# Hybrid decoder step: state, key, query and decay rows loaded through ScalarE's DMA queue

## The chip, the cores and the metric

The kernel runs on one core of a Trainium2 chip. The metric is the device time of one execution in microseconds (us); the median of the runs shown is compared. The engines are named as in the profile: PE (TensorE's matmuls), PEld (its weight loads), DVE (VectorE), ACT (ScalarE), POOL (GpSimd) and SP (SyncE, which here does nothing but issue DMAs). Each engine works through its own list of instructions in order; an instruction that waits for a semaphore holds everything behind it on that engine.

## What is computed

One layer of a decoder for 256 prompt positions and 8 sample sequences with one new token each (264 columns in all), followed by a final norm. Cut to what matters:

```python
h = rms_norm(x, norm_w)
z = h @ w_in                      # 4096 -> 14368 columns
# A: dilated window attention, 8 heads; B: trailing-mean pooling; C: gated delta rule, 16 heads
# C, prompt: chunked form, decay[i, j] = exp(gc[i] - gc[j]), gc = cumsum of the log decay
# C, sample: one step of the recurrence, for each of 8 samples and 16 heads
state = state * exp(g)
delta = (v - k @ state) * beta
state = state + outer(k, delta)
o     = q @ state
y = x + concat(A * silu(gA), B * silu(gB), C * silu(gC)) @ w_out
```

The caches and states are outputs too: the window cache is copied with one row replaced, and the new 128 x 128 state of each sample and head is written back.

## The kernel before

**The stream.** The 112 column tiles of `w_in`, a small one for the decays, and the 32 column tiles of `w_out` stream through PE one after the other. A chunk is 8 of a tile's 32 row blocks. Its weights arrive in one of three buffers `raw` (a load of 1 MB holds two chunks); ACT casts them to a high part `wh` (`emit_split`, L498, `s.copy`), DVE subtracts to get the low part `wl`, and PE runs three matmuls of 264 columns per row block (`emit_main`, L531, with the matmuls in L550 to L552), 24 for a chunk. There are four pairs `wh`/`wl` (`HB = 4`), so the cast for chunk n+3 stands in the program behind the matmuls of chunk n and waits until PE has left the buffer of chunk n-1. When DVE has read the last chunk of a `raw` buffer, the next load is put on SP's queue (`emit_loads`, L466), often followed by a piece of the cache copy, 512 KB from HBM to HBM (`emit_copy`, L486).

**The work beside it.** Everything else is written as Python generators that give up control at each `yield`: evacuations of finished tiles, the attention heads, the pooling, and of part C the keys' products (`kk`, L747), two `delta_worker`s that take the 16 prompt heads in turn (`delta`, L925), and two `sample_worker`s that take the 32 half heads of the samples (`sample`, L1063: four samples of one head each). Between two chunks `step` (L1417) picks the generators whose next piece fits, and the pieces' instructions are put into the engines' lists at that place. Matmuls of this side work are collected (`put`, L322) and given to PE in the middle of a chunk once they count as ready (`flush`, L330).

**The planner.** What fits is decided on a model of the engines' clocks (`Model`, L75; `Meter`, L144). It holds a time for PE, DVE, ACT, POOL and SP and one for the DMA engines, taken as one first-come queue (`Model.dma`, L132: SP gives 0.46 us to an issue, the transfer starts 0.65 us later at the earliest and behind all earlier ones, runs at 359 KB/us and counts as landed 0.9 us after its end). `ready` (L103) is the time at which an access's earlier readers and writers are done. The order of all engines' work is therefore fixed when the program is built.

**The loads of the change.** `send` (L298) yields until the model's time for the buffer and source is no later than PE's, then issues on SP:

```python
while not self.free and self.model.ready([out], [in_]) > self.model.t["pe"]:
    yield
self.sy.dma_start(out=out, in_=in_)
```

`load_decay` (L736) loads one head's row of `s_gc` to all 128 partitions (128 KB); `kk` uses it 16 times and `delta` 16 times. `sample` loads for each half head the states `sdT` (256 KB) into `Sb`, and a row of `s_k` and one of `s_q` to all partitions (256 KB each) into `kb` and `qb`. Each sample worker has one set of these buffers: a new state can only be loaded when the store `o_ds` of the previous one has landed, a new key row when DVE has read the last. After the loads, `due` (L293) yields until the model expects the last of them within 0.5 us; then come DVE's products with the keys. The stores (`o_ds`, `o_dp`, `s_q`), the weights, the copies and the attention's loads (`kg`, `vg`) also go through SP. All DMAs of SP and ACT share eight completion semaphores in turn, in the order of the program, and the framework lets an issue wait for the DMA that used its semaphore before.

Of the kernel before, what the change touches and what calls it, by code (L numbers as in the profile page):

```python
# [11 lines left out]
P = 128  # L12
NP = 256
# [177 lines left out]
class Builder:  # L191
# [106 lines left out]
    def send(self, out, in_):  # L298

        while not self.free and self.model.ready([out], [in_]) > self.model.t["pe"]:  # L300
            yield
        self.sy.dma_start(out=out, in_=in_)

    def pause(self, n):
        for _ in range(n):
            yield
# [427 lines left out]


    def load_decay(self, h, gcb):  # L736
        yield from self.send(gcb.ap, self.s_gc[h:h + 1, :].to_broadcast([P, NP]))

    def decay(self, h, gcb, D):

# [322 lines left out]
    def sample(self, h, f, Sb, kb, qb, jk, sm):  # L1063
        yield from self.wait(("q", h), ("v", h))
        n = NB // 2
        if f == 0:
            yield from self.send(self.s_q[h].rearrange("f d b -> d f b"),
                                 self.qall[:, h * NB:(h + 1) * NB].rearrange("d (f b) -> d f b", f=2))
        yield from self.send(Sb.ap, self.d["sdT"][h, :, f * 512:(f + 1) * 512])
        yield from self.send(kb.ap, self.s_k[h, f:f + 1].rearrange("f d b -> f (d b)").to_broadcast([P, 512]))  # L1070
        yield from self.send(qb.ap, self.s_q[h, f:f + 1].rearrange("f d b -> f (d b)").to_broadcast([P, 512]))
        yield from self.due(self.loaded)
        S = Sb.ap.rearrange("p (b k) -> p b k", b=n)
        k = kb.ap.rearrange("p (k b) -> p b k", b=n)
        q = qb.ap.rearrange("p (k b) -> p b k", b=n)
        junk = [jk.ap[:, i * P:(i + 1) * P] for i in range(4)]
        c0 = h * NB + f * n
        hs = slice(c0, c0 + n)
        eg, a1, a2 = (self.stab.ap[:, i * P + c0:i * P + c0 + n] for i in range(3))
        kS, dl = sm.ap[:, 0:n], sm.ap[:, n:2 * n]  # L1080
        for b in range(n):
            self.stt(junk[b], S[:, b], 1.0, k[:, b], ALU.mult, ALU.mult, accum=kS[:, b:b + 1])
            if b % 2:
                yield
                for j in (b - 1, b):
                    self.act(S[:, j], S[:, j], AF.Copy, scale=eg[:, j:j + 1])
        self.tt(dl, self.vall[:, hs], a2, ALU.mult)
        self.tt(kS, kS, a1, ALU.mult)
        self.tt(dl, dl, kS, ALU.subtract)
        yield  # L1090
        for b in range(n):
            self.stt(S[:, b], k[:, b], dl[:, b:b + 1], S[:, b], ALU.mult, ALU.add)
        yield
        for b in range(n):
            self.stt(junk[b], S[:, b], 1.0, q[:, b], ALU.mult, ALU.mult, accum=self.oall[:, c0 + b:c0 + b + 1])
        yield
        yield from self.send(self.d["o_ds"][h, :, f * 512:(f + 1) * 512], Sb.ap)
        self.ndone += 1
        if self.ndone == 2 * CH:
            self.start(self.sample_end())  # L1100
# [672 lines left out]
```

## Time and profile before

| | before |
|---|---|
| median of 3 runs | 1829.66 us (1829.58 to 1832.16) |
| the profiled execution | 1833.11 us |
| its span, first to last instruction | 1831.3 us |
| granted clock, mean share | 0.992 |
| PE busy | 1800.3 us (98%) |
| DVE / ACT / POOL busy | 1299.7 (71%) / 853.3 (47%) / 192.6 us (11%) |
| moved by the DMA engines | 519.13 MB, mean 283 GB/s |
| SP's hardware queue (q1) | 516.18 MB, 81.3% of the engines' time |
| ACT's hardware queue (q10) | 0.02 MB, 0.0% |

The page gives busy shares over the whole span. Where a stage lasted longer than its work is read from the windows, from the timeline of one engine (an idle time stands in brackets behind the instruction that ended it, with what it waited for), and from the lists of waits. SP is never counted as busy: its issues stand with the time that the issue took, and a wait of SP is one of its list.

### The profile page before, as it was taken

The page shows a single profiled execution, that of the slowest core. Times are in us where ns is not written, and L with a number is a line of the kernel's source. Part 1 is how long each engine was busy: PE and PEld are TensorE (multiplying, and loading weights), DVE is VectorE, ACT ScalarE, POOL GpSimd, SP SyncE. Part 2 cuts the span into 40 slices and gives each one's busy share as a digit, 9 for nine tenths or more (in the row PEclk, how much of TensorE's full clock was granted, in tenths as well). Part 3 has the DMA queues.
Part 4 walks back from the last instruction along what each step waited for, and adds up shares of the span by engine and source line. Part 5 has one row for each costly group of instructions (what it writes and reads, how often), then busy time and mean ns, then how long its engine had stood idle before and what let it go on. Part 6 is the DMA issues. An engine that isn't in the chain of part 4 may idle for free.

```text
span 1831.3 us, 38119 instructions
## 1 busy us (share of the span) xinstructions
PE 1800.3 (98%) x15122; PEld 1786.2 (98%) x15122; DVE 1299.7 (71%) x3157; ACT 853.3 (47%) x1439; POOL 192.6 (11%) x504
## 2 busy tenths in 40 slices
PE   9999999999999999999999999999999999999996
PEld 8999999999999999999999999999999999999995
DVE  7987889767888888888777876667655654444444
ACT  6744444445455555455544443444333444444442
POOL 1121454430111111110000000000000000000000
PEclk9999999999999999999999999999999999999998
DMA  8788778666889899889888887779888798888873
GB/s 305 267 313 281 266 247 240 232 205 226 277 269 326 287 300 306 291 293 297 313 304 319 323 293 270 287 277 344 313 296 288 264 344 306 305 296 308 298 241 118
DMA packets 109379, 519.13 MB, mean 283 GB/s; under 512 B 25408, under 2 KB 36256, under 8 KB 70272
## 3 DMA queue, kind: packets, MB, share of 16 engines
q1 hardware_dynamic: 108624, 516.18, 81.3%
q8 instruction: 118, 1.93, 0.4%
q0 software_dynamic: 432, 0.50, 0.1%
q14 instruction: 61, 0.50, 0.1%
q10 hardware_dynamic: 144, 0.02, 0.0%
HBM read 499.14 MB, written 152.50 MB: 356 GB/s over the span
## 4 chain that ended last, share of the span: by engine, by line
PE 83%; DVE 7%; DMA 7%; issue 1%; ACT 1%; SPq 1%; DVEq 0%; ACTq 0%
PE mps L550 25%; PE mps L551 25%; PE mps L552 25%; DVE arena L174 4%; PE sps L316 4%; DVE wl L174 2%; DMA o_ds<-arena 2%; DMA arena<-s_gc 1%; DMA raw<-win 1%; DMA arena<-vg 1%; PE sps L320 1%; PE sps L551 1%; PE sps L550 1%; PE sps L552 1%; SPq L158 1%
## 5 line engine op out<-in xcount | busy, mean ns | idle before, releaser
L550 PE MATMUL mps<-xh,wh 128*128 128x264 f32 x3456 | 998.6, 289 | 1.4 <-ACT wh L174 1.4
L551 PE MATMUL mps<-xl,wh 128*128 128x264 f32 x3456 | 982.3, 284 | 0.0
L552 PE MATMUL mps<-xh,wl 128*128 128x264 f32 x3456 | 981.5, 284 | 0.0
L174 DVE TENSOR_TENSOR wl<-raw,wh 128x1024 fp32r<-128x1024 f32 (+1 forms) x581 | 704.2, 1213 | 390.3 <-ACT wh L174 388.3
L174 ACT CAST wh<-raw 128x1024 fp32r<-128x1024 f32 (+1 forms) x581 | 603.6, 1040 | 601.4 <-PE mps L551 530.3
L550 PEld LDWEIGHTS mps<-xh,wh 128*128 128x128 f32 x3456 | 654.0, 189 | 4.7 <-ACT wh L174 2.7
L551 PEld LDWEIGHTS mps<-xl,wh 128*128 128x128 f32 x3456 | 653.5, 189 | 0.2
L552 PEld LDWEIGHTS mps<-xh,wl 128*128 128x128 f32 x3456 | 650.5, 188 | 0.2 <-DVE wl L174 0.2
L174 DVE SCALAR_TENSOR_TENSOR arena<-arena 128x128 f32<-128x128 f32 (+5 forms) x882 | 264.5, 354 | 22.1 <-DMA arena<-s_k 18.5
L174 ACT ACTIVATE arena<-arena 128x128 f32<-128x128 f32 (+6 forms) x319 | 118.7, 400 | 148.5 <-DVE arena L174 147.8
L550 PE MATMUL mps<-mixc,wh 128*128 128x264 f32 x512 | 145.5, 284 | 0.0
L550 PE MATMUL mps<-mix,wh 128*128 128x264 f32 x512 | 145.5, 284 | 0.0
L551 PE MATMUL mps<-mix,wh 128*128 128x264 f32 x512 | 145.1, 283 | 0.0
L551 PE MATMUL mps<-mixc,wh 128*128 128x264 f32 x512 | 145.1, 283 | 0.0
L552 PE MATMUL mps<-mixc,wl 128*128 128x264 f32 x512 | 145.0, 283 | 0.0
L552 PE MATMUL mps<-mix,wl 128*128 128x264 f32 x512 | 145.0, 283 | 0.0
L174 POOL COPY arena<-arena 128x8 f32<-128x8 f32 (+5 forms) x192 | 69.2, 380 | 462.3 <-DVE arena L174 377.1
L551 PEld LDWEIGHTS mps<-mixc,wh 128*128 128x128 f32 x512 | 96.5, 188 | 0.0
L551 PEld LDWEIGHTS mps<-mix,wh 128*128 128x128 f32 x512 | 96.5, 188 | 0.0
L550 PEld LDWEIGHTS mps<-mixc,wh 128*128 128x128 f32 x512 | 96.4, 188 | 0.0
L550 PEld LDWEIGHTS mps<-mix,wh 128*128 128x128 f32 x512 | 96.4, 188 | 0.0
L552 PEld LDWEIGHTS mps<-mix,wl 128*128 128x128 f32 x512 | 96.0, 187 | 0.0
(111 smaller groups left out, 1321.1 us busy)
## 6 DMA issues: line engine op xcount, KB each, us to landing
raw<-win SPq DMA_DIRECT2D x214, 1024.0 KB, 5.4
o_wk<-ck SPq DMA_DIRECT2D x128, 511.8 KB, 8.2
o_wv<-cv SPq DMA_DIRECT2D x128, 511.8 KB, 6.9
raw<-wout SPq DMA_DIRECT2D x58, 1024.0 KB, 5.4
arena<-kg SPq DMA_DIRECT2D x32, 320.0 KB, 7.0
arena<-vg SPq DMA_DIRECT2D x32, 320.0 KB, 8.0
arena<-sdT SPq DMA_DIRECT2D x32, 256.0 KB, 8.2
arena<-s_k SPq DMA_DIRECT2D x32, 256.0 KB, 7.8
```

What stands on the lines that cost most here:

```text
L158: return f(*a, **k)
L174: return f(*a, **k)
L316: self.put(lambda: self.t.matmul(out, lhsT=lhsT, rhs=rhs, start=start, stop=stop), out, [lhsT, rhs], 2)
L320: self.put(lambda: self.t.transpose(out, in_, self.ident[:k, :k]), out, [in_], 1)
L550: self.t.matmul(ps, lhsT=h[:, w], rhs=xh, start=(k == 0), stop=False)
L551: self.t.matmul(ps, lhsT=h[:, w], rhs=xl, start=False, stop=False)
L552: self.t.matmul(ps, lhsT=l[:, w], rhs=xh, start=False, stop=(k == NK - 1))
```

## The change

A new method `fetch` stands beside `send`. It yields under the same condition but issues on ACT's queue and keeps the model's books for that: ACT's clock goes to the time at which the buffer is ready plus 0.1 us, the transfer joins the model's one DMA queue as before, and `loaded` is the later of the queue's end plus 0.9 us and ACT's clock plus 4.0 us. `load_decay` and the three loads of `sample` call `fetch`; the store of `s_q` and all else stay on SP. The change touches 128 DMAs: 32 each of `s_gc`, `sdT`, `s_k` and `s_q`.

```diff
+    def fetch(self, out, in_):
+
+        m = self.model
+        while not self.free and m.ready([out], [in_]) > m.t["pe"]:
+            yield
+        self.s.dma_start(out=out, in_=in_)
+        m.t["s"] = max(m.t["s"], m.ready([out], [in_])) + .1
+        n = 4
+        for x in out.shape:
+            n *= x
+        m.t["dma"] = max(m.t["dma"], m.t["s"] + .65) + n / 359e3
+        self.loaded = max(m.t["dma"] + .9, m.t["s"] + 4.0)
+        m.done(self.loaded, [out], [in_])
 ...
     def load_decay(self, h, gcb):
-        yield from self.send(gcb.ap, self.s_gc[h:h + 1, :].to_broadcast([P, NP]))
+        yield from self.fetch(gcb.ap, self.s_gc[h:h + 1, :].to_broadcast([P, NP]))
 ...
-        yield from self.send(Sb.ap, self.d["sdT"][h, :, f * 512:(f + 1) * 512])
-        yield from self.send(kb.ap, self.s_k[h, f:f + 1].rearrange("f d b -> f (d b)").to_broadcast([P, 512]))
-        yield from self.send(qb.ap, self.s_q[h, f:f + 1].rearrange("f d b -> f (d b)").to_broadcast([P, 512]))
+        yield from self.fetch(Sb.ap, self.d["sdT"][h, :, f * 512:(f + 1) * 512])
+        yield from self.fetch(kb.ap, self.s_k[h, f:f + 1].rearrange("f d b -> f (d b)").to_broadcast([P, 512]))
+        yield from self.fetch(qb.ap, self.s_q[h, f:f + 1].rearrange("f d b -> f (d b)").to_broadcast([P, 512]))
```

## Rows read from the trace of the kernel before

**Rows 1.** The page, part 1: busy time, share of the span, instructions

```profile
PE 1800.3 (98%) x15122; PEld 1786.2 (98%) x15122; DVE 1299.7 (71%) x3157; ACT 853.3 (47%) x1439; POOL 192.6 (11%) x504
```

**Rows 2.** Windows: length, busy us (instructions) of five engines, PEclk, DMA share, GB/s

```profile
400.00:1000.00 600.00, 589.96 (x4871) 585.88 (x4870) 480.36 (x1429) 308.47 (x651) 54.77 (x163) 0.99 0.87 292
1400.00:1800.00 400.00, 400.00 (x3306) 399.73 (x3305) 205.04 (x241) 175.24 (x223) 0.00 (x0) 1.00 0.81 287
```

**Rows 3.** Timeline of PE: start, us, instruction [idle before, releaser], five places

```profile
436.93 0.49 PE L316 MATMUL sps<-arena 128*128 128x128 f32 x2 [0.65 <-DVE arena L174]
...
485.68 0.94 PE L316 MATMUL sps<-arena,kt 128*128 128x128 f32 x4 [3.18 <-ACT arena L174]
...
765.48 0.44 PE L320 MATMUL sps<-small,arena 128*128 128x128 f32 x2 [2.70 <-DVE arena L174]
...
875.97 0.53 PE L320 MATMUL sps<-small,arena 128*128 128x128 f32 x2 [0.62 <-DVE arena L174]
...
954.60 0.83 PE L320 MATMUL sps<-small,arena 128*128 128x128 f32 x3 [1.54 <-ACT arena L174]
```

**Rows 4.** Windows of 5 us behind the idle time at 485.68

```profile
485.00:490.00 5.00, 4.32 (x23) 4.32 (x24) 3.48 (x14) 3.30 (x10) 0.30 (x1) 0.66 0.33 92
490.00:495.00 5.00, 5.00 (x44) 5.00 (x44) 4.96 (x17) 3.41 (x7) 0.00 (x0) 1.00 0.77 295
```

**Rows 5.** Timeline of DVE: waits for loads, four places

```profile
431.18 1.14 DVE L174 SCALAR_TENSOR_TENSOR arena<-arena 128x128 f32<-128x128 f32 x4 [2.09 <-DMA arena<-s_gc]
...
483.32 0.38 DVE L174 SCALAR_TENSOR_TENSOR arena<-arena 128x128 f32<-128x128 f32 x1 [2.25 <-DMA arena<-s_k]
...
688.28 0.39 DVE L174 SCALAR_TENSOR_TENSOR arena<-arena 128x128 f32<-128x128 f32 x1 [2.14 <-DMA arena<-s_k]
...
761.34 0.39 DVE L174 SCALAR_TENSOR_TENSOR arena<-arena 128x128 f32<-128x128 f32 x1 [3.89 <-DMA arena<-s_k]
```

**Rows 6.** Waits: engine, line, releaser: us in total, times, longest

```profile
DVE arena L174 <- DMA arena<-s_k: 18.5, 13, 3.9
```

**Rows 7.** DMA issues: queue, count, KB each, median us from issue to landing

```profile
arena<-s_k SPq DMA_DIRECT2D x32, 256.0 KB, 7.8
...
arena<-cmask POOLq DMA_DIRECT2D x1, 64.0 KB, 10.4
```

**Rows 8.** SP's issues: ns min/median/max of the issue, first and last start

```profile
L158 SPq DMA_DIRECT2D arena<-s_gc x32: 319/572/1420, 115.8 to 805.2; - x32
L158 SPq DMA_DIRECT2D arena<-sdT x32: 328/388/1217, 415.9 to 978.7; - x32
L158 SPq DMA_DIRECT2D arena<-s_k x32: 320/455/1842, 416.6 to 979.7; - x32
L158 SPq DMA_DIRECT2D arena<-s_q x32: 319/430/1384, 424.2 to 980.9; - x32
```

**Rows 9.** Waits of SP for landings: us in total, times, longest

```profile
SPq L158 <- DMA raw<-win: 32.5, 27, 3.0
SPq L158 <- DMA o_ds<-arena: 25.1, 15, 6.5
...
SPq L158 <- DMA o_wk<-ck: 13.8, 14, 2.2
```

**Rows 10.** The chain that ended last: start, us, what

```profile
414.69 7.34 DMA o_wk<-ck
422.05 9.10 DMA arena<-s_gc
```

**Rows 11.** Waits of ACT: the longest in total

```profile
ACT wh L174 <- PE mps L551: 530.3, 330, 2.8
```

**Rows 12.** Timeline of SP and of ACT around one load of a state

```profile
744.09 0.58 SPq L158 DMA_DIRECT2D o_ds<-arena  x1
...
753.23 0.33 SPq L158 DMA_DIRECT2D arena<-sdT  x1
...
751.24 1.05 ACT L174 CAST wh<-raw 128x1024 fp32r<-128x1024 f32 x1 [1.85 <-PE mps L551]
```

## The prediction, made before the changed kernel ran

> **What bounds the kernel now.** I read the page first. PE is busy for 1800.3 of 1831.3 us [rows 1], so whatever the change does must show in PE's idle time or in the pace of its matmuls. Next come windows by stage, to find where PE is not busy. From 1400 to 1800 us, where only the stream is left, PE is busy for all of 400 us; from 400 to 1000 us, where the delta heads and the samples run beside the stream, it lacks 10.0 of 600 us [rows 2]. The rest of the missing time lies ahead of the first matmul and behind the last, where no load of the change runs. The third view is the timeline of PE between 400 and 1000 us. It shows that the 10 us are a few holes, and five of them make 8.7 us: 0.65 + 3.18 + 2.70 + 0.62 + 1.54 [rows 3]. Each ends at a small matmul of the side work that waits for DVE or ACT; none ends at a matmul that waits for weights. After a long hole there is a second loss: in the 5 us behind 485 us the granted clock is 0.66, that is the lower of the two levels (1.2 GHz) for about 3.4 us, after PE had stood idle for 3.18 us; PE finishes 23 matmuls there against 44 in the next 5 us [rows 4]. Of that, 0.68 us is still the hole, and 3.4 us at half speed cost 1.7 us more. The hole of 2.70 us at 765 us looks the same and is put at 1.7 us too.
>
> Then the timeline of DVE says why. DVE waited 2.25 us for a key row just ahead of the hole at 485.68, 3.89 us ahead of the one at 765.48, and 2.09 us for decays at 431.18, ahead of the one at 436.93 [rows 5]. In total DVE waited 18.5 us for key rows, in 13 waits [rows 6]. DVE is 80% busy in this stretch [rows 2], so a late load pushes everything behind it, and the planner has put a matmul in PE's list for a time that no longer holds. Not every wait costs: 2.14 us at 688.28 is followed by no hole [rows 3, 5].
>
> So what the change can win is bounded: the five holes and two slow stretches, 8.7 + 3.4 = 12.1 us, against 1833.11 us of the profiled execution (span 1831.3 and 1.8 us around it). That execution lies 3.4 us (0.19%) above the median of 1829.66 us, and I carry the difference over to the median.
>
> **The change part by part.** *The loads leave SP's queue.* A key row lands 7.8 us after its issue [rows 7], for 256 KB that at the mean 292 GB/s [rows 2] are 0.9 us of transfer; the rest is mostly time behind weights and copies that SP issued earlier. On ACT's queue they no longer stand in that line. How soon they then land no row shows. Bounds: not below about 1 us for the transfer itself; not above what the one row of a second queue shows beside a busy SP queue, 10.4 us for 64 KB [rows 7]. I take 5 to 6 us, between the ends, because the 7.8 us are the nearest row (same size, same form) and a load would pass part of that line. The waits to be removed are 2 to 4 us long, so two or three us suffice. *They can also be issued earlier.* SP reaches a place in the program after ACT does, since it first waits for DVE to release weight buffers. At 753.23 SP issued a state load; ACT had finished its work ahead of that place before the cast at 751.24, and stood idle 1.85 us [rows 12]. I count three quarters of the 12.1 us as won: **-9.0 us** (ends 0 and -12.1). What is late next is DVE itself, with 80% busy.
>
> *128 issues on ACT.* On SP an issue takes a median of 0.57, 0.39, 0.46 and 0.43 us for the four kinds [rows 8], together 32 x 1.85 = 59 us; at the maxima, 1.2 to 1.8 us, a group of three takes 4.4 us. ACT is busy for 308 of 600 us in the stretch [rows 2]. The model gives it 0.1 us for each, so some 1.0 us per group of three comes unplanned. The cover is ACT's wait for PE ahead of a cast, 530.3 us in 330 waits, 1.6 us each [rows 11]; three median issues (1.27 us) fit into it where no evacuation stands between. If they don't, a small matmul waits for the evacuation. I take **+1 us** (ends 0 and +5).
>
> *New waits on ACT.* The loads carry their waits with them. Behind a waiting issue stand the casts of the weights, so DVE's subtraction and the stream, and the evacuations that delta's next matmul waits for. Three kinds of wait come. One is the buffer: at 753.23 SP had waited for the store issued at 744.09 [rows 12]; ACT would have stood there too, and the cast of 751.24 would have come two us later or more. SP waited 25.1 us in 15 waits for such stores, the longest 6.5 us [rows 9]. The second is the completion semaphore: SP's decay load at 422.05 was released by the landing of a cache copy issued at 414.69 [rows 10], which nobody reads and which is the eighth issue before it. SP waited 32.5 us for landed weights and 13.8 us for copies, 41 waits [rows 9], mostly of this kind; the model knows nothing of them, and ACT, which comes to the place earlier than SP, meets them earlier. The third is DVE's last read of a key row; the model knows that, and `fetch` lets ACT's clock wait for it. What a held us costs has no row. Bounds: 0, as for the 2.14 us at 688.28; and 0.65, which is what DVE's 18.5 us of waits cost (12.1 / 18.5). ACT has more room than DVE, 49% idle against 20%, so I scale: 0.65 x 20 / 49 = 0.27 per us. The 25.1 us for stores would cost 6.7 us; the model foresees about half, since it too lets ACT wait for the modelled landing: **+3.4 us** (ends 0 and 0.27 x 71.4 = +19.3, all three waits of rows 9).
>
> *SP is relieved* of 59 us of issues and of the waits at them. Weights then go out a little earlier. No hole waited for weights [rows 3], so this counts 0. The s_q store stays on SP in front of a load on ACT; the order is kept by a wait, of the third kind. The bytes are the same, and the DMA engines have 13% left in the stretch [rows 2].
>
> *The order of the work changes.* The model moves every generator that comes after a changed `loaded`, so holes will not stand where they stood. I give this no sign; it adds some us to both sides of the range.
>
> **Sum:** -9.0 + 1 + 3.4 = -4.6 us: 1833.1 becomes 1828.5 for an execution like the profiled one, and the median 1829.66 becomes **1825.0 us**, 0.25% faster.
>
> **The rivals.** *The loads come no earlier* (no change). A load on ACT's queue shares the DMA engines, 87% busy [rows 2], and is held by the same buffers and semaphores. For it speaks the 64 KB on POOL's queue that took 10.4 us [rows 7]; against it that a lone row, for a software queue, decides little. Then the holes stay and the costs are small: -1 + 1 = 0, 1829.7 us. The Trainium skill, "DMA: Bandwidth & Descriptors", section "Issuing engines are not separate DMA queues", says that transfers from several engines run on the same 16 DMA engines and interleave, and that issuing from more of them saves only issue time; by that rule this rival holds, and the trace agrees as far as the POOL row goes. The same page, section "Queues, rings and completion order", lets each DMA engine take turns between the rings that have work, and by that the loads would pass part of SP's line; no row here shows ACT's ring under load.
>
> *ACT held* (slower). The waits of rows 9 now hold casts and evacuations. Place: 415 to 980 us, and at the densest where both sample workers load together. Price: 71.4 us x 0.27 = 19.3 us; less the 9.0 us won, +10 us: 1840 us. It decides as soon as a held us costs over 0.13 us (9.0 / 71.4). For it: the semaphore waits are unplanned. Against it: the casts are ready early, ACT waits for PE ahead of 330 of them [rows 11]. A milder form, half the price, is 1830 us, no change.
>
> *The change does not issue the loads earlier*, because ACT waits where SP waited: the first rival's time.
>
> **How the numbers follow.** A change under 0.2% (3.7 us) can't be told from none for this kernel. The forecast has 0.45, all of it faster by over 0.2%, 1816 to 1826 us; no change 0.28, from 1826 to 1833.3; ACT held 0.27, above. The lower end leaves out only a full win of all 12.1 us: 1817. The upper end takes in the slower case but for its upper part: 1838. Where the forecast holds, its own range is 1817 to 1826 us.
>
> **What would show it.** Right: 128 issues in ACT's queue, about 28 MB in its hardware queue; DVE's waits for key rows well below 18.5 us; landing times under 7.8 us; PE's holes between 400 and 1000 us down from 10 us to about 4, and no stretch of that part at the lower clock. Wrong: holes that end at evacuations by ACT, with ACT waiting in its queue for landings of stores, copies or weights for 40 us or more; casts that come so late that the stream's own matmuls wait; or landing times as before.

## The result and the profile after the change

| | before | after |
|---|---|---|
| median | 1830.91 us (4 runs) | **1856.14 us** (1852.61 to 1863.73, 4 runs) |
| ratio, 95% interval | | **1.0142** (1.0105 to 1.0179) |
| the profiled execution | 1833.11 us | 1863.73 us |
| PE idle in 400 to 1000 us | 10.0 us | 32.0 us |
| DVE's waits for the four kinds of load | 20.9 us in 15 | 3.5 us in 2 |
| ACT's idle time that ended at an issue or a landing | 10.9 us in 9 | 96.0 us in 30 |
| SP's waits for landings of these loads | 7.3 us in 13 | 128.1 us in 42 |

The change made the kernel 25 us slower; 4.6 us faster had been forecast. (The ratio is that of the means. The three rows of waits are sums over the lists of waits between 100 and 1040 us, each from one profiled execution; that of the changed kernel is the slowest of its four, 0.4% above their median.) The loads did move to ACT's queue, as the page's part on queues shows (packets, MB, share of the 16 engines):

```profile
q1 hardware_dynamic: 90192, 486.81, 74.7%
q10 hardware_dynamic: 18576, 29.38, 5.6%
```

The windows of after, beside [rows 2] and [rows 4], say where the time went: in the same 600 us PE gets through 4620 matmuls where it had done 4871, and behind a hole the granted clock is 0.50, the lower level.

```profile
400.00:1000.00 600.00, 568.02 (x4620) 562.02 (x4619) 456.71 (x1353) 290.99 (x625) 60.83 (x160) 0.98 0.83 274
520.00:525.00 5.00, 4.27 (x19) 3.97 (x20) 3.93 (x13) 0.87 (x3) 1.63 (x5) 0.50 0.76 247
```

PE is idle for 21.9 us more than before, and by the trace's record of the granted clock it runs at the lower level (half speed) for 23.9 us of this stretch instead of 6.8, which costs another 8.5. The sum, 30.5 us, is nearly the whole distance of 30.6 us between the two profiled executions. By the releasers, 14.7 of the 32.2 us of holes that PE has in its list of waits between 100 and 1040 us end at ACT, the others at DVE. The timeline of PE has more long holes than [rows 3]; four of them:

```profile
520.73 0.48 PE L334 MATMUL sps<-small,arena 128*128 128x128 f32 x1 [4.96 <-DVE arena L174]
...
595.33 0.58 PE L330 MATMUL sps<-arena,kt 128*128 128x128 f32 x1 [3.19 <-ACT arena L174]
...
683.61 0.55 PE L330 MATMUL sps<-arena 128*128 128x128 f32 x1 [2.45 <-ACT arena L174]
...
827.99 0.47 PE L334 MATMUL sps<-small,arena 128*128 128x128 f32 x1 [3.60 <-DVE arena L174]
```

The lists of waits of DVE, ACT and SP between 100 and 1040 us answer to [rows 6], [rows 11] and [rows 9] (us in total, times, longest):

```profile
DVE arena L174 <- DMA arena<-s_k: 3.5, 2, 3.0
...
ACT arena L174 <- issue: 30.9, 8, 8.0
ACT wh L174 <- issue: 20.2, 8, 8.2
...
ACT wh L174 <- DMA arena<-s_k: 9.1, 2, 5.5
ACT arena L174 <- DMA o_wk<-ck: 8.1, 2, 6.5
...
SPq L158 <- DMA arena<-s_gc: 60.5, 14, 9.2
SPq L158 <- DMA arena<-sdT: 38.0, 12, 17.2
...
SPq L158 <- DMA arena<-s_q: 22.4, 9, 4.3
...
SPq L158 <- DMA arena<-s_k: 7.2, 7, 3.6
```

In the same stretch of the kernel before, these were all the idle times of ACT that ended at an issue or a landing, and the largest of SP's waits for the four kinds of load:

```profile
ACT wh L174 <- issue: 7.8, 6, 1.4
...
ACT wh L174 <- DMA raw<-win: 3.1, 3, 1.5
...
SPq L158 <- DMA arena<-s_k: 2.9, 3, 1.3
```

DVE hardly waits for keys any more. In exchange ACT stands idle until issues have gone out, and, what the prediction did not have at all, SP stands waiting for loads that ACT issues. ("issue" is the page's word for idle time before which the engine waited for nothing that the profile shows; in the places below, issues of loads stand in it.) The row that names o_wk<-ck is to be read with care: its longest, 6.48 us up to 680.92, was a state load held until 678.16, and what had landed at 678.08 was the store o_ds issued at 669.89; the list names the copy that happened to land last.

Two pieces of the chain of waits show both kinds (start, us, what):

```profile
412.99 4.32 DMA arena<-s_k
...
417.38 0.34 SPq L158
...
418.34 9.75 DMA s_q<-small
...
428.17 0.33 ACTq L158
428.54 0.67 ACTq L158
...
429.25 0.38 ACT arena L174
...
429.67 0.71 PE sps L330 x4
...
805.82 9.24 DMA o_ds<-arena
...
815.08 0.34 ACTq L158
815.46 1.61 ACTq L158
...
817.16 1.43 ACTq L158
818.63 1.06 ACT wh L174
819.71 1.23 DVE wl L174
...
827.99 1.11 PE sps L334 x4
```

From 805.82 on it is ACT alone: the store of a state takes 9.24 us to land, ACT's next state load waits for it, the issues of key and query behind it take 1.61 and 1.43 us, and only then come the cast, behind the longest of ACT's idle times that ended at an issue (8.2 us), and DVE behind it. From 412.99 on it goes through both lists: ACT's key load has to land before SP may use its completion semaphore again (417.38), so SP issues the store of the queries late (418.34), ACT's query load waits for that store (428.17), and an evacuation and PE wait for ACT.

### The profile page after: what moved, and what is told of

Its sections match the earlier page's. It is cut to its first block, busy times and chain, and to the rows that moved or that the text cites. A ratio compares the mean times of both kernels' runs of the same rounds, so it can differ in the third digit from the quotient of the medians.

```text
span 1861.9 us, 38130 instructions
## 1 busy us (share of the span) xinstructions
PE 1808.6 (97%) x15122; PEld 1792.5 (96%) x15122; DVE 1299.6 (70%) x3157; ACT 849.6 (46%) x1439; POOL 201.5 (11%) x504
## 4 chain that ended last, share of the span: by engine, by line
PE 82%; DMA 8%; DVE 7%; ACT 1%; issue 1%; ACTq 1%; SPq 0%; POOL 0%; DVEq 0%; POOLq 0%
PE mps L564 25%; PE mps L565 25%; PE mps L566 24%; DVE arena L174 4%; PE sps L330 4%; DMA o_ds<-arena 4%; DVE wl L174 2%; DMA arena<-s_k 1%; PE sps L334 1%; ACTq L158 1%; PE sps L565 1%; PE sps L564 1%; PE sps L566 1%; ACT wh L174 1%; DMA s_q<-small 1%
## 5 line engine op out<-in xcount | busy, mean ns | idle before, releaser
L174 ACT CAST wh<-raw 128x1024 fp32r<-128x1024 f32 (+1 forms) x581 | 602.6, 1040 | 604.1 <-PE mps L565 484.7
L174 POOL COPY arena<-arena 128x3 f32<-128x3 f32 (+5 forms) x192 | 67.3, 370 | 466.9 <-DVE arena L174 434.9
```

The costliest lines, as they stand in the source:

```text
L174: return f(*a, **k)
```

## The experiments

| run | the 128 loads | ratio (95%) | SP's waits for ACT's DMAs | ACT idle until issue or landing | DVE's waits for loads | PE idle, 400 to 1000 |
|---|---|---|---|---|---|---|
| changed kernel | all on ACT | 1.0142 (1.0105-1.0179) | 128.1 | 96.0 | 3.5 | 32.0 |
| order_sp | SP, new order | 0.9998 (0.9983-1.0013) | 0 | 17.1 | 25.2 | 13.3 |
| queue_only | ACT, old books | 1.0159 (1.0139-1.0179) | 112.8 | 95.1 | 2.9 | 33.3 |
| kq_act | states on SP | 1.0166 (1.0147-1.0185) | 179.6 | 70.4 | 32.1 | 30.2 |
| state_act | states alone on ACT | 0.9996 (0.9984-1.0008) | 23.2 | 49.6 | 11.4 | 11.6 |
| decay_act | decays alone on ACT | 1.0122 (1.0097-1.0146) | 85.2 | 26.5 | 36.3 | 26.2 |
| samples_act | decays on SP | 1.0119 (1.0099-1.0139) | 41.2 | 73.6 | 2.4 | 24.8 |
| tiny_act | SP, 128 x 64 bytes on ACT | 1.0757 (1.0723-1.0791) | 262.2 | 57.0 | 114.2 | 86.3 |
| tiny_sp | SP, 128 x 64 bytes on SP | 1.0393 (1.0378-1.0409) | 0 | 28.1 | 62.4 | 52.2 |
| order_pool | all on POOL | 1.0070 (1.0046-1.0094) | 0 | 22.6 | 23.5 | 15.8 |
| decay_pool_same | decays alone on POOL | 1.0054 (1.0034-1.0074) | 0 | 25.2 | 24.0 | 15.4 |
| late_act | ACT, put later | 1.0089 (1.0061-1.0117) | 195.0 | 59.4 | 0.2 | 13.1 |
| kq_first | ACT, state last | 1.0128 (1.0107-1.0149) | 135.5 | 80.0 | 5.7 | 28.0 |
| soon | SP, due 2.5 us later | 0.9951 (0.9936-0.9966) | 0 | 10.4 | 2.5 | 4.2 |
| soon_state | states on ACT, due later | 0.9993 (0.9981-1.0006) | 15.7 | 50.7 | 0.3 | 12.6 |
| soon_after | ACT, due later | 1.0115 (1.0094-1.0137) | 139.5 | 82.2 | 0.0 | 25.4 |
| soon_more | SP, due 5 us later | **0.9917** (0.9900-0.9934) | 0 | 13.0 | 0.0 | 0.0 |

All ratios are to the kernel before, run beside; waits are in us, from the lists between 100 and 1040 us of one profiled execution of each run. For order_pool that was the fastest of five (1834.09 us, median 1839.81), so its row shows a milder case than its ratio. Where an expectation names 117.6 or 75 us, that was worked out otherwise, by pairing each issue with the semaphore it waits on and that semaphore's landings; the lists, which name the releaser that came last, give 128.1 for the first.

### Queue and order apart

The change does two things at once: another engine issues, and the planner books the loads otherwise, so all work gets another order. The first run keeps the new order and gives the issue back to SP; the second keeps the issue on ACT and the old books.

```diff
 # order_sp
-        self.s.dma_start(out=out, in_=in_)
+        self.nc.sync.dma_start(out=out, in_=in_)
 # queue_only
         self.s.dma_start(out=out, in_=in_)
-        m.t["s"] = max(m.t["s"], m.ready([out], [in_])) + .1
 ...
+        self.loaded = m.dma(out, in_)
```

> The changed kernel with its order of work kept for PE, DVE, POOL and ACT's own instructions, and with the 128 loads issued by SP again instead of ACT. It separates the planner's new order (and its later due time for the loads) from the queue. In the changed kernel ACT sat idle for 95.8 us between 100 and 1020 us until an issue or a landing, against 9.4 us in the kernel before; the profiled runs are 30.6 us apart. Theory A (ACT is held by the waits that the loads carry): these waits are back on SP, so ACT's idle time until an issue or a landing falls to about 10 us, PE's holes from 32.5 to about 10 us, and the time comes to 1824 to 1834 us, 0.996 to 1.002 of the kernel before. Rival C (the new order itself costs, whoever issues): it stays at 1850 to 1860 us, 1.010 to 1.016, with DVE or ACT late for the small matmuls as in the changed kernel.

> The 128 loads are issued by ACT, but the planner keeps the books as if SP issued them, so the order of all other work is that of the kernel before. Theory A (ACT is held by the waits that the loads carry): the loss is here too, and as the planner does not know of ACT's waits it is not smaller than in the changed kernel: 1.012 to 1.030 of the kernel before, ACT idle 80 us or more until an issue or a landing. Rival C (the new order costs): 0.997 to 1.003. Together with the run that has the new order on SP it makes a two by two table of queue and order.

The order alone costs nothing (0.9998), the queue alone costs the whole loss (1.0159). With the new order on SP, DVE waits 25.2 us for loads as before, so it is the queue too that makes the loads come in time. Rival C falls. Nor do the loads on ACT's queue slow the weights on SP's: worked out from the semaphores' updates, a weight load between 400 and 1000 us lands 7.0 us after its issue in the changed kernel (median), 7.4 in the kernel before.

### Which of the loads

Each run sends some of the four loads back through `send`, so the planner's order of work differs a little from run to run too:

```diff
 # kq_act: states back to SP; state_act: the three others; decay_act: the three of samples; samples_act: decays
-        yield from self.fetch(Sb.ap, self.d["sdT"][h, :, f * 512:(f + 1) * 512])
+        yield from self.send(Sb.ap, self.d["sdT"][h, :, f * 512:(f + 1) * 512])
```

> The changed kernel, but the 32 loads of states go through SP; the 96 loads of keys, queries and decays stay on ACT. Theory A1 (what holds ACT is the wait of a state load for the landing of the store that used its buffer; one such chain has a store issued at 805.82, landed after 9.24 us, the state load at 815.08 and the next cast at 818.63 after 8.19 us of idle time): without these the loss is gone for the most part, 0.997 to 1.005 of the kernel before, and ACT's idle time until an issue or a landing is 30 us or less. Rival B (each load holds ACT about alike, by its issue and by the completion semaphore that it shares with SP's DMAs): three quarters of the loss stay, 1.009 to 1.014, ACT idle about 70 us.

> The opposite part: only the 32 loads of states go through ACT, the 96 others through SP as before. Theory A1 (the wait for the store's landing): most of the loss is here, 1.008 to 1.015 of the kernel before, ACT idle 50 us or more until an issue or a landing. Rival B (each load alike): a quarter of it, 1.002 to 1.005, ACT idle some 25 us.

> Only the 32 loads of decays go through ACT; states, keys and queries go through SP as before. A decay's row waits for no store. In the changed kernel SP waited 58.2 us in 12 places for landings of decays on ACT. Theory E (coupling): SP's waits for landings on ACT are 30 us or more and the time is 1.003 to 1.008 of the kernel before. Rival S (waits for stores): 0.997 to 1.002.

> The 96 loads of the samples go through ACT, the 32 of decays through SP. Against the changed kernel this takes away the 58.2 us that SP waited for decays on ACT and leaves ACT's 75 us of waits for stores. Rival S (waits for stores, with the issues of key and query right behind them: 8 us in one piece at 513.51 and 818.63): 1.011 to 1.016 of the kernel before, as the changed kernel. Theory E (coupling): about half of the loss, 1.005 to 1.010, as SP's waits for landings on ACT halve.

My first theory, A1, does not explain the loss: without the states on ACT it is all there, and with the states alone there is none, although ACT then does wait for their stores (list of waits of state_act). That these waits cost nothing does not follow: DVE's waits for loads fall to 11.4 us in the same run, and soon_state below, where that gain is had already, puts the price of the waits at some 8 us.

```profile
ACT arena L174 <- DMA o_ds<-arena: 22.1, 8, 3.9
...
ACT wh L174 <- DMA o_ds<-arena: 10.8, 4, 3.5
```

Rival B does not fit either: the loss does not go with the number of loads. The decays alone, 32 loads that wait for no store and leave ACT's idle time at 26.5 us (10.9 before), cost 1.2%. What they do is hold SP (list of waits of decay_act):

```profile
SPq L158 <- DMA arena<-s_gc: 85.2, 18, 9.4
```

One place shows it. These are rows of the timelines of ACT, SP, DVE and PE of decay_act:

```profile
730.57 0.33 ACTq L158 DMA_DIRECT2D arena<-s_gc  x1
...
727.40 0.52 SPq L158 DMA_DIRECT2D o_wk<-ck  x1
737.43 0.33 SPq L158 DMA_DIRECT2D arena<-sdT  x1
737.81 0.44 SPq L158 DMA_DIRECT2D arena<-s_k  x1
...
742.71 0.38 DVE L174 SCALAR_TENSOR_TENSOR arena<-arena 128x128 f32<-128x128 f32 x1 [5.10 <-DMA arena<-s_k]
...
744.15 0.60 PE L330 MATMUL sps<-arena,kt 128*128 128x128 f32 x3 [2.93 <-ACT arena L174]
```

SP is free at 727.92. Its next issue, a state load, uses the semaphore of a decay load that stands eight places earlier in the program, but in ACT's list; ACT comes to it only at 730.57, and it lands at 737.37. SP stands for 9.5 us, the key row behind it is late, DVE waits 5.10 us, PE 2.93. So the two lists are tied: no DMA of either goes out before the one eight places earlier in the program has landed, in whichever list that stands. (With the DMAs of SP and ACT put in the order in which they take the semaphores, this holds for every one of them in every trace kept, without an exception.) The samples alone cost as much in the other way, with few waits of SP (41.2 us) and ACT idle for 73.6. The two halves, 1.2% each, make 1.4% together, so they do not add up; that the waits overlap is the likely reason, not shown.

### What the tie costs by itself

Here no load is moved. A copy of 64 bytes is added beside each, on ACT in one run, on SP in the other.

```diff
+        self.tiny, self.ntiny = self.drp.tile([P, 16], F32, name="tiny"), 0
 ...
-        self.s.dma_start(out=out, in_=in_)
+        self.nc.sync.dma_start(out=out, in_=in_)
+        self.nc.scalar.dma_start(out=self.tiny[self.ntiny:self.ntiny + 1, :], ...)   # tiny_sp: self.nc.sync
```

> The order of work of the changed kernel with the 128 loads on SP (which took 0.9998 of the kernel before), and beside each load a DMA of 64 bytes issued by ACT from one DRAM place to another that nobody reads. ACT gets the same count of issues as in the changed kernel, and its DMAs stand in the same eight completion semaphores between SP's, but none of them waits for a store, a key or a decay. The program does more than the kernel before only by these 128 copies of 64 bytes. Theory E (coupling: SP's next issues wait for the landing of ACT's DMAs, which ACT issues late, and ACT's for SP's; in the changed kernel SP waited 117.6 us for landings of ACT's loads, 19.6 us where only the states were on ACT): SP waits 60 us or more for ACT's DMAs, and the time is 1.006 to 1.016 of the kernel before. Rival S (the loss comes from the data that ACT's loads wait for, 75 us for stores o_ds and s_q): 0.998 to 1.003. Rival I (the issues themselves on ACT, 128 x 0.3 to 0.6 us): 0.3 to 0.6 us a piece, at most 1.004.

> The control for the run with the 128 copies of 64 bytes on ACT, which took 1.0757 of the kernel before with SP waiting 265.6 us for their landings: the same copies at the same places, but issued by SP right behind the load they stand beside. Count of DMAs, completion semaphores and order are as in that run; only the issuing engine of the 128 copies differs. Theory E (what costs is that two engines' lists are tied together by the completion semaphores): SP's own DMAs come one after the other anyway, so the time is 1.000 to 1.010 of the kernel before, from 128 more issues of some 0.4 us and somewhat more waiting for own landings. Rival N (it is the mere number of DMAs between the eight semaphores): 1.05 or more here too.

128 copies that nobody reads make the kernel 7.6% slower on ACT; the list of waits of tiny_act, here over the whole run:

```profile
SPq L158 <- DMA tiny<-ident: 220.8, 49, 16.1
...
SPq L309 <- DMA tiny<-ident: 65.3, 20, 7.9
```

The control misses its expectation: on SP they still cost 3.9%, where at most 1% had been expected and N wanted 5% or more. So there are two parts. A DMA more costs something wherever it stands. It takes one of eight semaphores for as long as it is under way, 7.0 us in the median even for 64 bytes (worked out from the semaphores' updates), and 0.6 us of SP's time for its issue; how the 3.9% divide between the two was not measured. The same DMA on another engine's list costs nearly as much again, 3.6% or about 67 us. Neither S nor I, which allowed 0.4% at most, explains that: ACT is idle for 29 us more than in tiny_sp, which even at the 0.27 us per us of the prediction makes 8 us. N holds for about half.

### An engine with semaphores of its own

POOL's DMAs use eight other semaphores, as the traces show. The order of all work is kept.

```diff
-        self.s.dma_start(out=out, in_=in_)
+        self.nc.gpsimd.dma_start(out=out, in_=in_)     # decay_pool_same: the samples' loads on SP
```

> The changed kernel with one difference: its 128 loads are issued by POOL instead of ACT, in the same order of work. POOL's DMAs have completion semaphores of their own, apart from those that SP and ACT share. Theory E (coupling): SP waits for no landing of a load of POOL and the time is 0.996 to 1.004 of the kernel before, if POOL (11% busy) can bear the waits and the issues. Rival: the loads off SP's queue cost by themselves, whoever issues, or POOL's own small operations, on which delta and kk wait, come late behind held loads: 1.008 to 1.016.

> The run with only the decays on ACT (1.0122 of the kernel before, SP waiting 83.3 us for their landings, no store in front of them), with the 32 loads issued by POOL in the same order of work. Theory E (coupling by the shared completion semaphores): 0.997 to 1.004. Rival (decays come too late or too early for the order of work that this planning gives, whoever issues): 1.008 to 1.014.

Both lie between the two answers. With nothing but the issuing engine changed, half of the loss goes, 1.0142 to 1.0070 and 1.0122 to 1.0054. The second pair is the cleaner one: ACT's idle time is the same in both (26.5 and 25.2 us), and what goes is SP's 85.2 us of waits, with 32 issues of ACT. What remains has a different look: SP waits for none of POOL's loads, but DVE waits 23.5 and 24.0 us for loads again. Why POOL's loads are not as early as ACT's, and what the remaining 0.5 to 0.7% is, stays open.

### ACT's waits for stores

The first run puts state and query loads into ACT's list 6 us later, when the store should have landed; the second puts the state behind key and query.

```diff
 # late_act (6.0 for states and queries)
-        while not self.free and m.ready([out], [in_]) > m.t["pe"]:
+        while not self.free and m.ready([out], [in_]) + late > m.t["pe"]:
 # kq_first: kb, qb, Sb instead of Sb, kb, qb
```

> The changed kernel, but the loads of states and queries are put into ACT's list only when the model's ready time lies 6 us behind PE's clock, because a store was seen to land 8.3 us (median) after its issue where the model counts on about 2 us. ACT then seldom waits for a store. Rival S (the loss comes from ACT waiting for stores): ACT's waits for stores fall from 75 to under 25 us and the time comes back to 0.996 to 1.004 of the kernel before. Theory E (coupling by the completion semaphores): the loads are still 128 of ACT's DMAs, SP still waits 80 us or more for their landings, and 1.007 to 1.014 stays.

> The changed kernel with the three loads of a half head in another order: key and query first, the state last. The state's wait for the store of the state before it then no longer has the issues of key and query (up to 1.6 and 2.5 us) behind it before ACT can go on. In the changed kernel ACT's idle pieces with an issue in them were 30 between 400 and 1040 us, 38.2 us of them in what was over 3 us in each; with the states alone on ACT that was 9.7 us, at no loss. Rival S (long pieces of ACT): the excess over 3 us falls to 25 us or less and the time by 0.3% to 0.8%, to 1.006 to 1.011 of the kernel before. Theory E alone: no change, 1.012 to 1.016.

Later issue takes ACT's idle time from 96.0 to 59.4 us and 0.5% off the loss, though SP waits longer than in the changed kernel (195.0 us); 0.9% stays, as E had it. So waits for stores seem to be a part, about a third; the intervals of the two runs overlap, and the work behind these loads is put later too. The other order of the three loads changes nothing that these intervals can tell (1.0128 against 1.0142): ACT's idle time only falls to 80.0 us, and it now waits somewhat longer for the stores of queries (7.8 us after 5.2). Rival S does not hold alone.

### The semaphores relaxed

```diff
-        self.sy.dma_start(out=dst[...], in_=src[...])
+        self.loaded = self.model.dma(out, in_)
+        self.nc.gpsimd.dma_start(out=out, in_=in_)      # emit_copy, in the changed kernel and in the one before
```

> The changed kernel with its 256 cache copies issued by POOL, whose DMAs have semaphores of their own, instead of SP; order of all other work unchanged. So fewer other DMAs stand between ACT's loads on the eight shared semaphores, and the DMA that a given SP issue waits for is an older one. ACT still waits for the stores of states. Theory E (SP held at semaphores by ACT's loads; 117.6 us in the changed kernel): that wait falls to under 50 us, and against the same edit of the kernel before (copies_before) the change costs 0.7% or less. Rival S (ACT held at stores, with key and query issues behind): the change costs 1.2% or more against copies_before, with ACT idle as before.

> The kernel before with its 256 cache copies issued by POOL: the base for copies_after, so that what the copies do by themselves is taken out. No theory hangs on its own time; 0.99 to 1.01 of the kernel before.

The base missed its expectation badly: copies on POOL cost 1.0883 (1.0857 to 1.0909), with PE short of work between 1040 and 1800 us. On that base the change costs 0.6% (2006.02 against 1993.42 us), with SP's waits for ACT at 40.7 us and ACT idle for 84.8. That agrees with E and speaks against S alone, but on a kernel so disturbed the size can't be taken from it.

### The gain by itself

The term of the prediction that was to win was tried without any change of queue: work behind a load is planned later.

```diff
-SOON = 0.5
+SOON = -2.0        # soon_more: -4.5; soon_state and soon_after: the same in those kernels
```

> The kernel before, with one constant changed: the work behind a load is put in place 2.5 us later than the model's landing (due time 2.0 us behind it instead of 0.5 us ahead). It measures the gain term of the prediction without any change of queue: DVE waited 18.5 us for key rows and 25.5 us for loads in all between 100 and 1040 us, and these late loads were held to cost PE 12.1 us. If they do, DVE's waits for loads fall under 8 us, PE's holes between 60 and 1800 us from 10.1 to 6 us or less, and the time is 0.994 to 0.998 of the kernel before. Rival (a DVE that is not kept waiting here is late elsewhere, the holes do not hang on these waits): 0.998 to 1.004 with DVE's waits gone.

> States alone on ACT (0.9996 of the kernel before) with the due time 2.5 us later (which alone took 0.9951). If ACT's queue gives something beyond the due time, 0.990 to 0.994; if the 38 us that ACT waits for stores cost what they hold, 0.996 to 1.000; if neither, 0.994 to 0.996 like the due time alone.

> The changed kernel with the due time 2.5 us later. In the changed kernel DVE waits only 3.5 us for key rows, so late loads are no longer what PE waits for. If the loss comes from the waits of ACT and SP for each other (ACT idle 96 us until an issue or a landing, SP held 117.6 us by ACT's loads), these stay within a third of that and the time stays at 1.008 to 1.015 of the kernel before. Rival (late loads are still a part of it): 1.002 or less.

> The kernel before with the due time 5.0 us later than it was, twice the step that took 0.9951. DVE's waits for loads were already down from 25.5 to 6 us by the first step, PE's holes to 4.2 us and the clock's two low stretches gone, so at most 0.2% is left: 0.993 to 0.997. If the samples' work, put later, collides with other side work, 0.997 to 1.003.

With DVE's waits for loads down from 20.9 to 2.5 us the time falls by 9 us (0.9951), and PE lacks 4.2 us instead of 10.0. The next step beats its expectation: 1814.96 us against 1830.33 beside it, and PE is never idle in the stretch and runs at the upper level of its clock throughout:

```profile
400.00:1000.00 600.00, 600.00 (x5001) 599.05 (x5000) 488.03 (x1430) 311.32 (x641) 58.30 (x163) 1.00 0.86 297
```

In the changed kernel the later due time mends little (1.0115): its loads are not late. And it gives ACT's waits a price: states on ACT, where due times leave little else to win, take 0.9993 instead of 0.9951, 7.7 us for 40.3 us more of ACT's idle time, 0.19 us per us (0.10 to 0.28 by the two intervals). SP's 15.7 us of waits for these loads are in that price.

## Why the prediction was wrong

**The bound and the holes were read rightly.** Late key rows, DVE behind them, five holes and the clock were what could be won: taking the late loads away by the due time alone gave 9 us, the -9.0 of the sum. That it fits so closely is luck, as the three quarters were a guess. The bound of 12.1 us was a little low; soon_more won 15.4.

**Loads leave SP's queue (-9.0).** The waits went as told, 20.9 to 3.5 us. The reason was not mainly a faster landing of the keys. Worked out from the semaphores' updates a key row lands 7.2 us after its issue (7.9 before), a state 5.6 (6.9), a decay 5.0 (7.4), a query 8.5 (8.0); I had taken 5 to 6. Nor do the runs bear out that a key row's 7.8 us were mostly time behind what SP had issued earlier: in tiny_act 64 bytes on ACT's queue were under way for 6.2 us. The Trainium skill, "DMA: Bandwidth & Descriptors", section "Issuing engines are not separate DMA queues", says that issuing from several engines saves only issue time. The landings of keys and queries go with that, those of decays and states, 2.4 and 1.3 us sooner, do not, so they do not decide between this rule and the turns between rings that the prediction takes from the same page. What helped the keys more is the earlier issue: against order_sp, which has the same order of work, a key row goes out 1.3 us earlier (median, at the same place of PE's stream) and lands 0.4 us faster. That the 9 us are contained in the 25 lost, so that the costs come to some 34 us, is argued from soon, not shown.

**128 issues on ACT (+1).** Their sum is 75 us on ACT against 70 on SP, with up to 2.46 us for one. They hurt where they stand behind a wait (815.46 and 817.16 above). Not measured alone: tiny_act has as much, 74 us of issues, but SP's 262.2 us of waits with it.

**New waits on ACT (+3.4).** The price was fair, the amount was not. 0.27 us per us was estimated; soon_state gives 0.19, and late_act about 0.27 (9.7 us for 36.6 us less, with 1 to 18 us allowed by the intervals). But I let half of 25.1 us count, and ACT was idle 85 us longer than before. I had put the reason down myself: ACT comes to the place earlier than SP and so meets the stores earlier. I then charged it with SP's waits. The end of the range, 71.4 us, was the nearer figure, and the rival "ACT held" had the right sign and a price near what was measured; its condition, over 0.13 us per us, was met by both figures.

**SP is relieved (0).** This is the step that failed outright. I wrote that SP's and ACT's DMAs share eight semaphores in program order and followed it in one direction only, ACT waiting for SP's. The other direction, SP waiting for a load that stands in ACT's list behind casts and evacuations, did not occur to me; I even counted SP as freed. SP waited 128 us for such loads. In decay_act it waited 85.2 us, and the run lost 22.4 us; decay_pool_same, with the same order of work and none of these waits, still lost 10, so the waits account for 12 to 22 us, 0.15 to 0.26 per us. "No hole waited for weights" was true and beside the point: what is late behind SP's wait are the stores and loads of the samples. In the direction that I did follow, the pairing of issues and landings finds almost nothing: where ACT waited at a semaphore, some 7.5 us in all, it was for an earlier load of its own.

Both taken at these prices, 85 x 0.19 and 128 x 0.15 to 0.26, come to 35 to 49 us, where there are some 34. But the price of SP's waits is no constant: late_act has 195.0 us of them and loses 16 us in all, or some 25 with the 9 us of gain added. The waits of the two lists feed each other, as at 412.99, so the two do not simply add up. How the loss divides is not settled, and neither is what POOL's runs still lose.

**The order changes (no sign).** Right: 0.9998 with the new order on SP.

**What was to show it.** DVE's waits, the count of issues and the 28 MB came as told; so did the first sign that had been named for a wrong forecast, holes at ACT's evacuations with ACT waiting over 40 us. The range, up to 1838, left this case's size out, because the worst case was built from SP's waits of before, a list in which two engines do not yet wait for each other.

## What to carry to other kernels

When DMAs of two engines share completion semaphores, moving some of them to a second engine can make the first engine wait for the second's progress, as SP did here for 128 us: ask not only what the new issuer will wait for, but who will wait for the landing of what now stands in its list. Waits read off one engine's list are no measure of what another engine will meet there, as it comes to the place at another time. And where work only starts before its data has landed, try first to plan it later: one constant gave 0.8% here, the queue lost 1.4%.

## What the runs showed of the hardware

A copy of 64 bytes from DRAM to DRAM was under way for 7.0 us in the median on SP's queue and 6.2 on ACT's, about as long as a load of 256 KB on SP in the same two runs (medians 6.6 to 8.3 us). With eight semaphores for everything that SP and ACT issue, 128 such copies on SP cost 71 us, 0.56 us each; the issue of one took 0.6 us. In the changed kernel the lower level of PE's clock stood behind five of the six holes of 2.4 us or more (429.67, 520.73, 595.33, 683.61 and 827.99; not behind 2.65 us at 756.38), for 3.4 us or twice that.
